# The beginning of mixer 1 in a two-layer hybrid backbone: the context's norm at other points, rotary sums in PSUM, eight scalings left out, one query copy moved

## The chip, the core and the metric

The kernel runs on one core of one Trainium2 chip. The core has a matrix engine (PE), a vector engine (DVE), a scalar engine (ACT), a general engine (POOL) and a sync engine (SP) that here issues the transfers from HBM. Each engine runs its own instructions in order and waits on semaphores for the others. SBUF holds the operands; PE writes into eight PSUM banks, which DVE and ACT read. The metric is the device time of one execution in microseconds, taken as the median of several runs; lower is better.

## The reference, cut to what matters

512 latent tokens and 256 context tokens of width 1024 pass two layers; each layer is half a SwiGLU, a token mixer and half a SwiGLU again, every one of them modulated and closed by a layer norm. Mixer 1 is windowed attention with 16 query heads, 4 key heads and rotary positions. Its context tokens give keys and values only: behind this mixer nothing reads them.

```python
def window_gqa(u_lat, u_ctx, w_qkv, w_o, sinks, with_ctx_out):
    qkv = u_lat @ w_qkv
    q = axial_rope(qkv[..., :dq].reshape(B, S, N_HEADS, HEAD_DIM)) * scale
    k = axial_rope(qkv[..., dq:dq + dkv].reshape(B, S, WA_KV_HEADS, HEAD_DIM))
    v = qkv[..., dq + dkv:].reshape(B, S, WA_KV_HEADS, HEAD_DIM)
    kvc = u_ctx @ w_qkv[:, dq:]
...
    # per block of 128 queries: softmax over a window of 384 keys, all 256 context keys and a sink
...
# in reference(), for layer i = 1 (ctx_needed is False):
        h_lat = ffn_sublayer(h_lat, m_lat[0], m_lat[1], m_lat[2], ffn_w_in[i, 0], ffn_w_out[i, 0], ln_g[i, 0], ln_b[i, 0])
        h_ctx = ffn_sublayer(h_ctx, m_ctx[0], m_ctx[1], m_ctx[2], ffn_w_in[i, 0], ffn_w_out[i, 0], ln_g[i, 0], ln_b[i, 0])
        u_lat = modulate(h_lat, m_lat[3], m_lat[4])
        u_ctx = modulate(h_ctx, m_ctx[3], m_ctx[4])
        y_lat, y_ctx = window_gqa(u_lat, u_ctx, wa_w_qkv[j], wa_w_o[j], wa_sinks[j], ctx_needed)
        h_lat = layer_norm(ALPHA * h_lat + m_lat[5] * y_lat, ln_g[i, 1], ln_b[i, 1])
        h_lat = ffn_sublayer(h_lat, m_lat[6], m_lat[7], m_lat[8], ffn_w_in[i, 1], ffn_w_out[i, 1], ln_g[i, 2], ln_b[i, 2])
```

## The kernel before

Activations lie transposed: `z[d]` holds 128 of the 1024 channels for all 768 tokens, latent columns 0 to 511, context columns 512 to 767. What a product reads is split in two parts, a high one (`uh`, `wh`) and the rest (`ul`, `wl`); a product of exact numbers is three PE products of such parts (`mm3`, L163, L165, L166). Weights come as quarters of 128x512: SP loads one into `wr` (five buffers), ACT casts it into `wh` (L102), POOL subtracts into `wl` (L104).

The functions that the change touches are in `wa_mixer` and before it. The value and key products of the latent tokens (`vw`, `wk`) run over the eight channel tiles, and the name `wa_0` to `wa_7` marks the end of each. Then `query` makes two products of the first unit (`wq0_0`, `wq0_1`); `scaled` copies a bank into SBUF on ACT (`qe`). `turned` does the rotation: PE multiplies `qe` with a permutation (`pr`, L1129), DVE multiplies that with the sines (`sn`, L1131), POOL multiplies `qe` with the cosines (L1132), DVE adds (L1133). `stack_k` and `stack_q` copy the result on ACT and make the remainder on DVE: for the keys L868, L869, L870, L871, for the queries L861, L862. Then come the context's keys (`wkc`) and values (`vw` with `wh_0b` and so on), and the first query product of the next unit (named `early` in the code, `wq_0` in the profile again). `attn` makes the scores (`sw` and `sc`, L875 and L876), their minimum on DVE (L1217, L1220) and the exponential on ACT (L1232).

The norm that feeds this mixer is `l3`: `l3[0]` for the latent tokens, `l3[1]` for the context. It has seven parts: sums, mean, centers, variance (`pvl`, L475), spreading (`prl`, L403), out (the scaled tokens: `ufl` L318, `uh` L320, L322 or L324, `ul` L325) and kept (POOL scales `z` for the residual, L339). `plan` hangs parts on named points, and `at` runs them when the program gets there. With `firm`, the first product issued behind a variance or a spreading is held behind it on PE.

A scheduler that lays out its own timeline sets the order of each engine's instructions from this program, the dependencies, the buffers and PSUM banks that come free, and orders that `behind` fixes by hand. The banks are named by tags: two each of `mm`, `s` and `c`, one each of `t` and `o`. So an instruction can move though its line was not touched.

Of the kernel before, what the change touches and what calls it, by code (L numbers as in the profile page):

```python
# [37 lines left out]
def hybrid_kernel(ctx: ExitStack, tc: tile.TileContext, h0, cc, crow, wmod, wmodt, bmod, lnp, wst,  # L38
# [129 lines left out]
    def mmk(ps, w, m0, c0, c1, k0=0):  # L168

        for k in range(DT):  # L170
            kk = (k + k0) % DT
            mm3(ps, kw(w, kk, m0, m0 + P), [t[kk][:, c0:c1] for t in (uh, ul)], k == 0, k == DT - 1)

# [691 lines left out]
    def stack_k(k0, k1, kl0, kl1, c0, c1, src):  # L865

        for k, kl, own, other in ((k0, kl0, LOW, HIGH), (k1, kl1, HIGH, LOW)):
            nc.scalar.copy(k[own, c0:c1], src[own, :])  # L868
            nc.scalar.copy(k[other, c0:c1], src[own, :])  # L869
            nc.vector.tensor_tensor(out=kl[own, c0:c1], in0=src[own, :], in1=k[own, c0:c1].bitcast(F32), op=ALU.subtract)  # L870
            nc.scalar.copy(kl[other, c0:c1], kl[own, c0:c1].bitcast(F32))  # L871
# [232 lines left out]
    def wa_mixer(gt):  # L1104
# [15 lines left out]
        def scaled(nm, ps, scale, tag="t2"):  # L1120

            qe = t2(f"qe{nm}", tag)
            nc.scalar.activation(qe[:], ps[:], AF.Copy, scale=scale)
            return qe

        def turned(nm, qe):

            pr = bank("mm", f"pr{nm}")
            nc.tensor.matmul(pr[:], rm_sb[:], qe[:], start=True, stop=True)  # L1129
            sn = t2(f"sn{nm}")  # L1130
            nc.vector.tensor_tensor(out=sn[:], in0=pr[:], in1=rc[1][:], op=ALU.mult)  # L1131
            nc.gpsimd.tensor_tensor(out=qe[:], in0=qe[:], in1=rc[0][:], op=ALU.mult)  # L1132
            nc.vector.tensor_tensor(out=sn[:], in0=qe[:], in1=sn[:], op=ALU.add)  # L1133
            return sn

        def stacked_q(nm, qe):
            sl = [ph["S"].tile([P, NL], F32R, tag="wq", name=f"w{nm}_{x}", bufs=6) for x in range(2)]
            stack_q(*sl, 0, NL, turned(nm, qe), 1.0)
# [19 lines left out]
        def query(u, wq, i, tag="t2"):  # L1158
            ps = bank("mm", f"wq{u}_{i}")
            mmk(ps[:], wq, i * P, 0, NL)  # L1160
# [16 lines left out]
        for i in range(2):  # L1177
            stack_k(*ks[i], 0, NL, turned(f"k{i}", kes[i]))
        qes.append(query(0, wq, 1))
        qs = [stacked_q("q0_0", qes[0])]  # L1180
        for i in range(2):
            ps = bank("s", f"wkc{i}")
            mmk(ps[:, :NC], w, i * P, NL, NT)
            if i == 0:
                qs.append(stacked_q("q0_1", qes[1]))
            stack_k(*ks[i], NL, NT, ps[:, :NC])
# [214 lines left out]
    l3 = [ln("l3", i, g, 1, 0, 1, 3, "o", firm=i == 0, alone=i == 1) for i, g in enumerate(g2)]  # L1401
# [15 lines left out]
    plan(wa_4=l3[1][1:3], wa_7=l3[1][3:4], wq0_0=l3[1][4:6], wq0_1=l3[0][6:] + l3[1][6:])  # L1417
# [131 lines left out]
```

## Time and profile before

| | us |
|---|---|
| median of 3 runs | 2731.77 |
| the runs | 2731.77, 2726.20, 2731.79 |
| the profiled execution, its own time | 2735.21 |
| its span in the trace | 2733.4 |
| mean granted PE clock | 0.988 |

The page's first part gives the busy time of each engine; its second part cuts the span into 40 slices of 68 us and gives the busy share in tenths. Mixer 1 begins at about 2042 us, where the latent tokens' norm is done, and its first exponential starts at 2112.97 us. In these 71 us the views by order of time show each instruction with its start, its length, its tiles, and in brackets how long its engine had been idle before it and which instruction ended that.

### The profile page before, as it was taken

The numbers are of one execution on the slowest core, as the hardware profiler recorded it, in microseconds if no ns is written. First come the engines' busy times: TensorE is split into PE (matmuls) and PEld (weight loads), VectorE is DVE, ScalarE is ACT, GpSimd is POOL, SyncE is SP. The second block draws the span as 40 slices with busy tenths as digits, with TensorE's granted clock in tenths as the row PEclk, the third lists the DMA queues.
The fourth block names the chain that finished last, engine by engine and source line by source line (L and its number), as shares of the span: only waits on it lengthen the run. The fifth ranks groups of instructions, "written<-read, shape, count | busy, mean of one in ns | idle before, by whom it ended". The sixth has DMA issues, their size and how long they took to land.

```text
span 2733.4 us, 47740 instructions
## 1 busy us (share of the span) xinstructions
PE 2635.5 (96%) x16858; PEld 2406.7 (88%) x16858; DVE 1834.8 (67%) x4268; ACT 1206.9 (44%) x2505; POOL 1667.7 (61%) x1523
## 2 busy tenths in 40 slices
PE   7999999999999899999999999999998999899997
PEld 5799999888888889999998899999987777899997
DVE  4877777775555687556556676666577767687765
ACT  5244343266446353443433534343336655454542
POOL 4786767464444567867664577767645545577762
PEclk9999999999999999999999999999999999999998
DMA  9367565422222222454543226456632111245551
GB/s 332 94 176 197 140 164 166 145 78 67 59 59 63 59 61 83 132 130 121 128 130 101 69 82 160 125 150 173 200 115 62 32 32 43 66 105 128 135 143 59
DMA packets 295759, 311.90 MB, mean 114 GB/s; under 512 B 27873, under 2 KB 194017, under 8 KB 294497
## 3 DMA queue, kind: packets, MB, share of 16 engines
q1 hardware_dynamic: 279104, 279.36, 34.3%
q0 software_dynamic: 16128, 29.37, 6.4%
q8 instruction: 133, 2.18, 0.3%
q14 instruction: 106, 0.86, 0.1%
q10 hardware_dynamic: 288, 0.14, 0.0%
HBM read 300.92 MB, written 12.25 MB: 115 GB/s over the span
## 4 chain that ended last, share of the span: by engine, by line
PE 56%; DVE 6%; ACT 2%; issue 1%; DMA 1%; POOL 0%; DVEq 0%; SPq 0%; ACTq 0%; POOLq 0%
PE pd0b L165 2%; PE pd0b L163 2%; PE pd0b L166 2%; PE pd1a L163 2%; PE pd1a L165 2%; PE pd1a L166 2%; PE pd1b L163 1%; PE wo L909 1%; PE pd1b L165 1%; PE pd1b L166 1%; DVE z L503 1%; PE tpw L899 1%; PE sw L875 0%; PE wq L163 0%; PE wq L166 0%
## 5 line engine op out<-in xcount | busy, mean ns | idle before, releaser
L104 POOL TENSOR_TENSOR wl<-wr,wh 128x512 fp32r<-128x512 f32 x200 | 261.5, 1323 | 161.3 <-ACT wh L102 88.9
L104 POOL TENSOR_TENSOR wl_s<-S,wh_s 128x512 fp32r<-128x512 f32 x240 | 316.6, 1354 | 48.9 <-ACT wh_s L102 48.5
L102 ACT CAST wh_s<-S 128x512 fp32r<-128x512 f32 x256 | 155.2, 620 | 424.3 <-POOL S L644 140.9
L644 POOL TENSOR_TENSOR S<-wr,wr 128x512 f32<-128x512 f32 x128 | 173.9, 1359 | 187.3 <-DMA wr<-in_wst_dram 170.9
L211 DVE CUSTOM_DVE_ANT_0 jk<-wt,cb 128x512 f32<-128x512 f32 x360 | 244.6, 679 | 22.5 <-DMA wt<-in_wmodt_dram 18.2
L104 POOL TENSOR_TENSOR wl_a<-wr,wh_a 128x512 fp32r<-128x512 f32 x144 | 189.0, 1359 | 18.9 <-ACT wh_a L102 16.7
L102 ACT CAST wh_a<-wr 128x512 fp32r<-128x512 f32 x192 | 119.2, 622 | 155.3 <-PE pd1b L165 20.8
L102 ACT CAST wh<-wr 128x512 fp32r<-128x512 f32 x200 | 121.1, 617 | 108.0 <-DMA wr<-in_wst_dram 17.2
L503 DVE SCALAR_TENSOR_TENSOR z<-pd0b,gt,z 128x256 f32<-128x256 f32 (+1 forms) x168 | 96.7, 594 | 38.2 <-PE pd0b L166 37.9
L503 DVE SCALAR_TENSOR_TENSOR z<-pd1a,gt,z 128x512 f32<-128x512 f32 (+1 forms) x150 | 88.6, 605 | 37.4 <-PE pd1a L166 36.6
L918 POOL TENSOR_SCALAR p<-p,l 128x512 f32<-128x512 f32 x64 | 44.3, 694 | 102.3 <-DVE l L1025 95.3
L503 DVE SCALAR_TENSOR_TENSOR z<-pd0a,gt,z 128x512 f32<-128x512 f32 (+1 forms) x160 | 93.6, 611 | 15.7 <-PE pd0a L166 15.4
L644 POOL TENSOR_TENSOR S<-wr,S 128x512 f32<-128x512 f32 x64 | 90.3, 1411 | 3.4
L644 POOL TENSOR_TENSOR S<-S,wr 128x512 f32<-128x512 f32 x64 | 90.1, 1407 | 2.9
L339 POOL TENSOR_SCALAR z<-z,ag_None,ab_None 128x256 f32<-128x256 f32 (+1 forms) x77 | 59.2, 772 | 51.6 <-DVE uh L324 32.8
L918 POOL TENSOR_SCALAR pw<-pw,l 128x512 f32<-128x512 f32 (+1 forms) x64 | 42.6, 666 | 71.4 <-DVE l L1246 41.7
L1024 ACT ACTIVATE p<-s,m 128x512 f32<-128x512 f32 x64 | 44.0, 688 | 77.8 <-DVE m L1021 70.7
L325 DVE TENSOR_TENSOR ul<-ufl,uh 128x256 fp32r<-128x256 f32 (+1 forms) x88 | 61.7, 708 | 6.0 <-ACT uh L320 3.5
L503 DVE SCALAR_TENSOR_TENSOR z<-pd1b,gt,z 128x512 f32<-128x512 f32 (+1 forms) x91 | 53.2, 618 | 9.7 <-PE pd1b L166 8.2
L318 ACT ACTIVATE ufl<-z,bi_None,sc_None 128x256 f32<-128x256 f32 (+1 forms) x77 | 48.1, 637 | 25.2 <-DVE z L488 24.9
L104 DVE TENSOR_TENSOR wl_a<-wr,wh_a 128x512 fp32r<-128x512 f32 x48 | 51.6, 1086 | 6.3 <-ACT wh_a L102 6.3
L163 PE MATMUL vn<-wh,uh 128*128 128x256 f32 x192 | 54.7, 285 | 1.1 <-DVE nq L862 0.6
(1479 smaller groups left out, 10579.1 us busy)
## 6 DMA issues: line engine op xcount, KB each, us to landing
wr<-in_wst_dram SPq DMA_DIRECT2D x456, 256.0 KB
wt<-in_wmodt_dram SPq DMA_DIRECT2D x206, 256.0 KB
wr_0b<-in_wst_dram SPq DMA_DIRECT2D x47, 256.0 KB
wr_1b<-in_wst_dram SPq DMA_DIRECT2D x47, 256.0 KB
wr_2b<-in_wst_dram SPq DMA_DIRECT2D x47, 256.0 KB
wr_3b<-in_wst_dram SPq DMA_DIRECT2D x47, 256.0 KB
wm<-in_wmod_dram SPq DMA_DIRECT2D x8, 1024.0 KB
zspare<-in_wmodt_dram SPq DMA_DIRECT2D x30, 256.0 KB
```

The source lines that it names most:

```text
L102: nc.scalar.copy(hi[:], src[:])
L104: x = eng.tensor_tensor(out=lo[:], in0=src[:], in1=hi[:].bitcast(F32), op=ALU.subtract)
L163: behind(nc.tensor.matmul(ps, a[0], b[0], start=first, stop=False), in_front[0])
L165: nc.tensor.matmul(ps, a[0], b[1], start=False, stop=False)
L166: last_pe[0] = nc.tensor.matmul(ps, a[1], b[0], start=False, stop=last)
L211: x = nc.vector.tensor_tensor_reduce(out=junk[:], in0=w[:], in1=cb[st], scale=1.0, scalar=0.0, op0=ALU.mult, op1=ALU.add, accum_out=out[st])
L318: nc.scalar.activation(uv, zs, AF.Identity, scale=s1, bias=s2)
L325: return hi, nc.vector.tensor_tensor(out=lo, in0=uv, in1=uo.bitcast(F32), op=ALU.subtract)
L339: nc.gpsimd.tensor_scalar(out=zs, in0=zs, scalar1=prm[2][:, d:d + 1], scalar2=prm[3][:, d:d + 1], op0=ALU.mult, op1=ALU.add)
L503: last[0] = nc.vector.scalar_tensor_tensor(out=zt(d, c0, c1), in0=pd, scalar=gt[:, d, st:st + 1], in1=zt(d, c0, c1), op0=ALU.mult, op1=ALU ...
L644: nc.gpsimd.tensor_tensor(out=t[:], in0=a[:], in1=b[:], op=o)
L918: nc.gpsimd.tensor_scalar(out=p, in0=p, scalar1=r, scalar2=0.0, op0=ALU.mult, op1=ALU.add)
```

## The change

In four places the program is changed. `mmk` marks a point behind each of the eight channel tiles of a product, so that a plan can name them. The context's norm `l3[1]` is issued at `wa_3` (mean, centers), `wa_6` (variance) and `wq0_0_4` (spreading, out) in place of `wa_4`, `wa_7` and `wq0_0`, and it is `firm` now; its last part, the eight scalings of the context's `z`, is left out, as nothing reads them. `turned` may be given a bank: then the permuted tile is taken in that bank and DVE leaves the product and the sum there. The two keys use `t` and `c`, the first unit's two queries `mm`. And the copy in `scaled` is held on ACT behind the last copy of `stack_k`, when there is one, which concerns the next unit's query.

```diff
@@ -165,11 +165,12 @@
         nc.tensor.matmul(ps, a[0], b[1], start=False, stop=False)
         last_pe[0] = nc.tensor.matmul(ps, a[1], b[0], start=False, stop=last)
 
-    def mmk(ps, w, m0, c0, c1, k0=0):
+    def mmk(ps, w, m0, c0, c1, k0=0, nm=None):
 
         for k in range(DT):
             kk = (k + k0) % DT
             mm3(ps, kw(w, kk, m0, m0 + P), [t[kk][:, c0:c1] for t in (uh, ul)], k == 0, k == DT - 1)
+            at(f"{nm}_{k}")
 
 
     def gemv(layer, ch, pieces, tag):
@@ -868,7 +869,8 @@
             nc.scalar.copy(k[own, c0:c1], src[own, :])
             nc.scalar.copy(k[other, c0:c1], src[own, :])
             nc.vector.tensor_tensor(out=kl[own, c0:c1], in0=src[own, :], in1=k[own, c0:c1].bitcast(F32), op=ALU.subtract)
-            nc.scalar.copy(kl[other, c0:c1], kl[own, c0:c1].bitcast(F32))
+            x = nc.scalar.copy(kl[other, c0:c1], kl[own, c0:c1].bitcast(F32))
+        return x
 
     def scores(ps, q, k, kl, qc, kc):
 
@@ -1120,22 +1122,24 @@
         def scaled(nm, ps, scale, tag="t2"):
 
             qe = t2(f"qe{nm}", tag)
-            nc.scalar.activation(qe[:], ps[:], AF.Copy, scale=scale)
+            behind(nc.scalar.activation(qe[:], ps[:], AF.Copy, scale=scale), last_k[0])
             return qe
 
-        def turned(nm, qe):
-
-            pr = bank("mm", f"pr{nm}")
+        def turned(nm, qe, room=None):
+
+            pr = bank(room or "mm", f"pr{nm}")
             nc.tensor.matmul(pr[:], rm_sb[:], qe[:], start=True, stop=True)
-            sn = t2(f"sn{nm}")
+            sn = pr if room else t2(f"sn{nm}")
             nc.vector.tensor_tensor(out=sn[:], in0=pr[:], in1=rc[1][:], op=ALU.mult)
             nc.gpsimd.tensor_tensor(out=qe[:], in0=qe[:], in1=rc[0][:], op=ALU.mult)
             nc.vector.tensor_tensor(out=sn[:], in0=qe[:], in1=sn[:], op=ALU.add)
             return sn
 
-        def stacked_q(nm, qe):
+        last_k = [None]
+
+        def stacked_q(nm, qe, room=None):
             sl = [ph["S"].tile([P, NL], F32R, tag="wq", name=f"w{nm}_{x}", bufs=6) for x in range(2)]
-            stack_q(*sl, 0, NL, turned(nm, qe), 1.0)
+            stack_q(*sl, 0, NL, turned(nm, qe, room), 1.0)
             return sl
 
         iv = wpos[0]
@@ -1157,7 +1161,7 @@
 
         def query(u, wq, i, tag="t2"):
             ps = bank("mm", f"wq{u}_{i}")
-            mmk(ps[:], wq, i * P, 0, NL)
+            mmk(ps[:], wq, i * P, 0, NL, nm=f"wq{u}_{i}")
             at(f"wq{u}_{i}")
             return scaled(f"q{u}_{i}", ps, -0.125, tag)
 
@@ -1175,15 +1179,15 @@
         wq = wunit()
         qes = [query(0, wq, 0)]
         for i in range(2):
-            stack_k(*ks[i], 0, NL, turned(f"k{i}", kes[i]))
+            stack_k(*ks[i], 0, NL, turned(f"k{i}", kes[i], "tc"[i]))
         qes.append(query(0, wq, 1))
-        qs = [stacked_q("q0_0", qes[0])]
+        qs = [stacked_q("q0_0", qes[0], "mm")]
         for i in range(2):
             ps = bank("s", f"wkc{i}")
             mmk(ps[:, :NC], w, i * P, NL, NT)
             if i == 0:
-                qs.append(stacked_q("q0_1", qes[1]))
-            stack_k(*ks[i], NL, NT, ps[:, :NC])
+                qs.append(stacked_q("q0_1", qes[1], "mm"))
+            last_k[0] = stack_k(*ks[i], NL, NT, ps[:, :NC])
         wv = wunit(again=iv)
         for j in (4, 5):
             context_v(j)
@@ -1398,7 +1402,7 @@
     l0 = [ln("l0", i, g, 0, 0, 0, 3, "o", firm=i == 0, alone=i == 1) for i, g in enumerate(g2)]
     l1 = [ln("l1", i, g, 0, 1, 0, 6, ("mm", "t", "o")[i], held=False, pool=i == 0) for i, g in enumerate(g3)]
     l2 = [ln("l2", i, g, 0, 2, 1, 0, "o", True, firm=i == 0) for i, g in enumerate(g2)]
-    l3 = [ln("l3", i, g, 1, 0, 1, 3, "o", firm=i == 0, alone=i == 1) for i, g in enumerate(g2)]
+    l3 = [ln("l3", i, g, 1, 0, 1, 3, "o", firm=True, alone=i == 1) for i, g in enumerate(g2)]
     l4 = [ln("l4", i, g, 1, 1, 1, 6, ("mm", "o")[i]) for i, g in enumerate(g1)]
 
     ffn("0a", g2, lambda: gate(0, 2, 0.5), late_gate, whole(l0[0], l0[1][:1]), first,
@@ -1414,7 +1418,7 @@
     gemv_dve(1, (24, 40, (0, 1)), (40, 72, (0,)))
     plan(pa1a_0_0_0=l2[0][6:], pa1a_0_1_0=l2[1][1:3], pd1a_0_0_1=l2[1][3:4], pd1a_0_0_4=l2[1][4:])
     ffn("1a", g2, lambda: gate(1, 2, 0.5), None, whole(l3[0], l3[1][:1]), apart=True)
-    plan(wa_4=l3[1][1:3], wa_7=l3[1][3:4], wq0_0=l3[1][4:6], wq0_1=l3[0][6:] + l3[1][6:])
+    plan(wa_3=l3[1][1:3], wa_6=l3[1][3:4], wq0_0_4=l3[1][4:6], wq0_1=l3[0][6:])
     plan(wo6_2=l4[0][:1], wo6_3=l4[0][1:2], wm7_3=l4[0][2:3], wo7_3=l4[0][3:4] + [lambda: back(last_rstd[0])],
          pow3_1_256_2=[lambda: back(None)] + l4[0][4:6], pow3_1_256_7=l4[1][:1])
     wa_mixer(gate(1, 5, 1.0))
```

The diff shifts the line numbers: a line of the program before is one to four higher in the changed one (L1129 is L1131 there, L861 is L862, L475 is L476). What the change makes of the order, on two engines. On PE at the first key's rotation, before: `wq_0` is the first query's product, `prk` the two keys' rotations.

```order
L166 MATMUL wq_0_23085<-uh_106,wl_2_23076 128x512
L475 MATMUL pvl_1_23025<-onesd,aql_1_1_22948 128x1 x2
L163 MATMUL wq_0_23085<-uh_107,wh_3_23081 128x512
L165 MATMUL wq_0_23085<-ul_115,wh_3_23081 128x512
L166 MATMUL wq_0_23085<-uh_107,wl_3_23082 128x512
L163 MATMUL wq_0_23085<-uh_108,wh_3_23081 128x512
L165 MATMUL wq_0_23085<-ul_116,wh_3_23081 128x512
L166 MATMUL wq_0_23085<-uh_108,wl_3_23082 128x512
L1129 MATMUL prk_23155<-qek_23049,rm_sb 128x512
L1129 MATMUL prk_23169<-qek_23051,rm_sb 128x512
L163 MATMUL wq_1_23183<-uh_101,wh_0_23063 128x512
```

And after, at the first key's rotation, which now stands ahead of the first query's products:

```order
L166 MATMUL wk_22847<-uh_108,wl_3_22839 128x512
L476 MATMUL pvl_1_23007<-onesd,aql_1_1_22930 128x1 x2
L163 MATMUL vw_22842<-wh_3_22814,uh_108 128x256
L165 MATMUL vw_22842<-wl_3_22815,uh_108 128x256
L166 MATMUL vw_22842<-wh_3_22814,ul_116 128x256
L1131 MATMUL prk_23155<-qek_23049,rm_sb 128x512
L163 MATMUL wq_0_23085<-uh_101,wh_0_23063 128x512
L165 MATMUL wq_0_23085<-ul_109,wh_0_23063 128x512
```

The first rotation stands ahead of all 24 products of the first query in place of behind them; the variance `pvl` stands ahead of the last three value products. The second key's rotation follows 15 query products later, and the spread (`prl`) 15 after that.

On ACT behind the last context token (`uh_108`), up to the copies of the context's keys (`wk` and `wkl` out of `wkc`), before; `wq` out of `snq` are query copies, `qeq` is the next unit's query.

```order
L102 CAST wh_3_23414<-wr_3_23412 128x512
L318 ACTIVATE ufl_1_7_23149<-z_99,bi_0_1_3_None,sc_0_1_3_None 128x256
L322 ACTIVATE uh_108<-z_99,bi_0_1_3_None,sc_0_1_3_None 128x256
L102 CAST wh_0_23964<-wr_0_23962 128x512
L102 CAST wh_1_23970<-wr_1_23968 128x512
L1123 ACTIVATE qeq_0_23443<-wq_0_23418 128x512
L868 CAST wk_0_23041<-wkc_23238 64x256
L869 CAST wk_0_23041<-wkc_23238 64x256
L102 CAST wh_2_23976<-wr_2_23974 128x512
L868 CAST wk_1_23045<-wkc_23283 64x256
L869 CAST wk_1_23045<-wkc_23283 64x256
```

And after, at the same place:

```order
L323 ACTIVATE uh_108<-z_99,bi_0_1_3_None,sc_0_1_3_None 128x256
L102 CAST wh_2_23396<-wr_2_23394 128x512
L102 CAST wh_3_23402<-wr_3_23400 128x512
L862 ACTIVATE wq_0_0_23216<-prq_0_23218 64x512
L102 CAST wh_0_23952<-wr_0_23950 128x512
L102 CAST wh_1_23958<-wr_1_23956 128x512
L862 ACTIVATE wq_0_1_23217<-prq_0_23218 64x512
L869 CAST wk_0_23041<-wkc_23227 64x256
L862 ACTIVATE wq_1_0_23252<-prq_1_23254 64x512
L870 CAST wk_0_23041<-wkc_23227 64x256
L102 CAST wh_2_23964<-wr_2_23962 128x512
L869 CAST wk_1_23045<-wkc_23271 64x256
```

The next unit's query (`qeq`) no longer stands ahead of the context's keys, and the first unit's query copies, which stood ahead of the last context tokens, stand among the weight casts behind them.

On PE at the end of the context's products, before: `wkc` and `vw` are the context's keys and values, `wq_0` is the next unit's first query.

```order
L165 MATMUL vw_23367<-wl_3b,uh_108 128x256
L166 MATMUL wq_0_23418<-uh_107,wl_3_23415 128x512
L163 MATMUL wq_0_23418<-uh_108,wh_3_23414 128x512
L165 MATMUL wq_0_23418<-ul_116,wh_3_23414 128x512
L166 MATMUL wq_0_23418<-uh_108,wl_3_23415 128x512
L165 MATMUL wkc_23238<-ul_116,wh_3_22838 128x256
L166 MATMUL wkc_23238<-uh_108,wl_3_22839 128x256
L165 MATMUL wkc_23283<-ul_116,wh_3_22838 128x256
L166 MATMUL wkc_23283<-uh_108,wl_3_22839 128x256
L166 MATMUL vw_23340<-wh_3b,ul_116 128x256
L166 MATMUL vw_23367<-wh_3b,ul_116 128x256
L875 MATMUL sc_1_0_23508<-wk_0_23041,wq_0_0_23226 128x256
```

And after:

```order
L165 MATMUL vw_23328<-wl_3b,uh_108 128x256
L166 MATMUL vw_23328<-wh_3b,ul_116 128x256
L166 MATMUL vw_23355<-wh_3b,ul_115 128x256
L163 MATMUL vw_23355<-wh_3b,uh_108 128x256
L165 MATMUL vw_23355<-wl_3b,uh_108 128x256
L166 MATMUL vw_23355<-wh_3b,ul_116 128x256
L163 MATMUL wq_0_23406<-uh_101,wh_0_23384 128x512
L165 MATMUL wq_0_23406<-ul_109,wh_0_23384 128x512
L166 MATMUL wq_0_23406<-uh_101,wl_0_23385 128x512
```

The 24 products of that query stood among the context's products and now stand behind all of them. In the last FFN, where the same norm helper serves the latent tokens, the scheduler has moved one spread (`prl`) ahead of 12 products; no line of it was changed.

## The prediction, made before the changed kernel was run

> **What bounds the kernel now.** I read the totals by engine first, then the busy time in stretches of 10 us over the beginning of mixer 1, then the order of time of PE, ACT, DVE and POOL there.
>
> ```profile
> PE 2635.5 (96%) x16858; PEld 2406.7 (88%) x16858; DVE 1834.8 (67%) x4268; ACT 1206.9 (44%) x2505; POOL 1667.7 (61%) x1523
> ...
> 2080.00:2090.00 10.00, 7.02 (x32) 5.16 (x31) 9.07 (x15) 9.77 (x18) 7.08 (x7) 0.83 0.30 78
> ...
> 2100.00:2110.00 10.00, 6.59 (x37) 5.27 (x36) 5.44 (x8) 6.04 (x16) 7.44 (x6) 1.00 0.45 132
> 2110.00:2120.00 10.00, 7.47 (x27) 6.01 (x26) 7.41 (x30) 6.83 (x20) 2.42 (x4) 0.50 0.07 26
> ```
>
> A stretch's row gives busy us of PE, weight loads, DVE, ACT and POOL, then the granted clock. PE is busy 96% of the span, so only places where it waits can be won, and these three stretches are such a place: PE 7.02, 6.59 and 7.47 of 10, ACT at 9.77 in the first, and the clock down to 0.83 and 0.50. The waits themselves (start, us, idle before and releaser in brackets):
>
> ```profile
> 2072.44 1.98 PE L1129 MATMUL prk<-qek,rm_sb 128*128 128x512 f32 x4
> ...
> 2078.49 0.60 PE L403 MATMUL prl<-idn,yl 128*128 128x128 f32 x4
> ...
> 2085.31 0.38 PE L165 MATMUL wkc<-ul,wh 128*128 128x256 f32 x1 [2.92 <-DVE ul L325]
> ...
> 2086.56 0.41 PE L163 MATMUL vw<-wh_0b,uh 128*128 128x256 f32 x1
> 2086.77 0.41 PE L165 MATMUL vw<-wl_0b,uh 128*128 128x256 f32 x1
> ...
> 2090.31 0.28 PE L165 MATMUL vw<-wl_1b,uh 128*128 128x256 f32 x1
> 2090.43 0.28 PE L163 MATMUL vw<-wh_1b,uh 128*128 128x256 f32 x1
> ...
> 2104.49 0.40 PE L166 MATMUL vw<-wh_3b,ul 128*128 128x256 f32 x2
> 2105.50 0.38 PE L875 MATMUL sc<-wk,wq 128*128 128x256 f32 x1 [0.61 <-ACT wk L869]
> 2108.12 0.38 PE L876 MATMUL sc<-wkl,wq 128*128 128x256 f32 x1 [2.24 <-ACT wkl L871]
> ...
> 2113.80 0.69 PE L875 MATMUL sw<-wk,wq 128*128 128x384 f32 x1 [1.97 <-ACT pw L1232]
> ```
>
> Two waits matter. At 2085.31 the context's products stop 2.92 us for the context's normed tokens; afterwards equal products start 0.21 us apart instead of 0.12, the halved clock. From 2104.9 the first scores wait, step after step, for ACT's copies of the context's keys. ACT's rows say why those are late:
>
> ```profile
> 2076.67 0.62 ACT L868 CAST wk<-snk 64x512 fp32r<-64x512 f32 x1 [0.29 <-DVE snk L1133]
> 2077.32 0.62 ACT L869 CAST wk<-snk 64x512 fp32r<-64x512 f32 x1
> ...
> 2099.07 1.39 ACT L102 CAST wh<-wr 128x512 fp32r<-128x512 f32 x2 [0.81 <-PE wkc L165]
> 2104.22 0.60 ACT L1123 ACTIVATE qeq<-wq 128x512 f32<-128x512 f32 x1 [3.77 <-PE wq L166]
> ...
> 2109.94 0.87 ACT L871 CAST wkl<-wkl 64x256 fp32r<-64x256 f32 x2
> 2111.67 1.28 ACT L1232 ACT_TABLE_LOAD   x1 [0.86 <-DVE m L1220]
> 2112.97 0.69 ACT L1232 ACTIVATE pw<-sw,m 128x512 f32<-128x512 f32 x1
> ```
>
> From the first key cast (2076.67) to the last (2110.8) ACT waits only twice, 0.81 and 3.77 us. ACT is the bound of this stage; the 3.77 us are the query copy that stood ahead of the key copies while its products were not done. I take the exponential at 2112.97 as the stage's end.
>
> **The change, step by step.** All times on the clock of before.
>
> *Rotated keys.* They now start as soon as their product is there:
>
> ```profile
> 2066.01 1.29 ACT L1123 ACTIVATE qek<-wk 128x512 f32<-128x512 f32 x2
> ...
> 2066.28 0.39 PE L166 MATMUL wk<-uh,wl 128*128 128x512 f32 x1
> 2066.51 0.39 PE L163 MATMUL wq<-uh,wh 128*128 128x512 f32 x1
> ...
> 2073.54 2.55 POOL L1132 TENSOR_TENSOR qek<-qek,rc 128x512 f32<-128x512 f32 x2 [6.16 <-PE prk L1129]
> ...
> 2073.50 0.69 DVE L1131 TENSOR_TENSOR snk<-prk,rc 128x512 f32<-128x512 f32 x1 [0.41 <-PE prk L1129]
> ...
> 2075.06 3.28 DVE L1133 TENSOR_TENSOR snk<-qek,snk 128x512 f32<-128x512 f32 x2
> ```
>
> PE spends 0.23 us on a product of 512 columns (2066.28 to 2066.51), 0.12 on one of 256. Three value products move behind the keys, so the first key's last product starts at 2066.28 - 0.36 - 0.69 = 2065.2 and ends at 2065.6; ACT's copy (1.29/2) ends at 2066.3; PE meanwhile does the second key (0.69), the variance (0.3) and three value products (0.36) and comes to the rotation at 2066.8, unhindered. Rotation 1.0, POOL's product 1.28, DVE's sum and three handovers of 0.1 follow. The sum took 1.64 us (3.28/2) with both operands in SBUF; the row at 2073.50, with one operand in PSUM and POOL busy beside it, took 0.69. With the sum left in PSUM I take 0.69, and 1.64 as the other end. ACT's first key cast: 2070.2 instead of 2076.67, **6.5 us earlier** (5.5 by the other end).
>
> *ACT's chain.* It lasted 2110.8 - 2076.7 = 34.1 us. Out go both waits (4.6) and the query copy (0.5); in come a weight cast that stood ahead (0.65, a cast's pitch from 2076.67 to 2077.32) and one wait for DVE's residual, as the first key's low copy now stands directly behind its casts:
>
> ```profile
> 2078.26 1.40 DVE L870 TENSOR_TENSOR wkl<-snk,wk 64x512 fp32r<-64x512 f32 x2
> ```
>
> That is 1.40/2 + 0.05 = 0.75. So 30.4 us, and its end at 2100.6, 10.2 earlier. Reading PSUM rather than SBUF could change its 12 rotated casts and copies by 0.05 us each either way: 0 taken, +-0.6 as bounds.
>
> *The context's norm.* Its variance comes at about 2066.2 on PE, and its reciprocal root, which ended at 2074.3 (first row below), some 4 us earlier. PE goes: first rotation done 2067.8, 30 query products (6.9), second rotation (1.0), so the spread at 2075.7 instead of 2078.49, not waiting; 18 more query products (4.1) and the spread (0.4): context at 2080.2, its first low half needed six products later, at 2080.9.
>
> ```profile
> 2074.11 0.15 DVE L367 SCALAR_TENSOR_TENSOR yl<-pvl,yl 128x2 f32<-128x2 f32 x1
> ...
> 2083.71 1.54 DVE L325 TENSOR_TENSOR ul<-ufl,uh 128x256 fp32r<-128x256 f32 x1 [0.83 <-ACT ufl L318]
> ...
> L339 POOL TENSOR_SCALAR z<-z,ag_None,ab_None x8: 659/874/1240, 2085.0 to 2100.8; 128x256 f32<-128x256 f32 x8
> ```
>
> Ahead of the context's first scaling ACT has 13 casts (13 x 0.64) and the 0.75: 2079.3, scaled 2079.8; DVE's last key residual and the low half (0.7 + 0.4, or 1.54 as in its row) end at 2080.6 to 2081.7. PE waits 0 to 0.8 us here instead of 2.92; I take 0, as POOL has no work then. The 96 products (11.5) and two rotations (1.9) run at full clock to 2093.6. POOL's eight unread scalings (8 x 0.87 = 7.0 us) go; nothing waited for them, so 0, at best what they held up on DVE.
>
> *The new wait.* The first query's sum now stays in the bank that the next query's 24 products need; they wait for DVE's second residual of it. ACT ends the last context token at 2090.2 by its chain, then come two weight casts, a query copy, two weight casts, a query copy: 6 x 0.64, 2094.1; DVE 0.7: 2094.8. **PE waits 1.2 us**; queued behind are those 24 products (5.5), ending at 2100.3, then the scores (12 x 0.12 and a drain): 2102.
>
> *The first exponential.* DVE's new order puts both heads' masks ahead of both minima:
>
> ```profile
> 2111.87 0.49 DVE L1217 CUSTOM_DVE_ANT_0 sw<-sw,mk,nsink 128x256 f32<-128x256 f32 x1 [0.28 <-PE sw L876]
> ```
>
> So one mask, one minimum (0.5 each) and reads (0.3) behind the scores, 2103.3; table load 1.28: 2104.6 against 2112.97. **-8.4 us.** Behind it the order is the old one, and PE at 96% with weights fetched on request carries the shift to the end.
>
> *A second place.* In the last FFN the same norm helper's spread moves ahead of 12 products (1.4 us):
>
> ```profile
> 2362.17 0.60 PE L403 MATMUL prl<-idn,yl 128*128 128x128 f32 x4
> ...
> 2364.71 0.39 PE L163 MATMUL pa1b<-uh,wh 128*128 128x256 f32 x1 [1.22 <-ACT uh L320]
> ```
>
> The 1.22 us wait that follows should mostly go: -1.0, between -1.2 and +0.3 (if the root isn't ready).
>
> Sum -9.4 us. Of the profiled execution's 2735.21 (span 2733.4 and 1.8 around it) that leaves 2725.8. That execution lies 3.4 us above the median 2731.77; on the median **2722.4**. What a measurement of this kernel can tell from no change is about 0.2%, 5.5 us.
>
> **Rivals.**
>
> *Carried only in part.* For: ACT has no slack between 2070 and 2100, so whatever it waits for adds in full. Weight quarters are asked for when POOL is done with the fifth one before, and took 3.2 us:
>
> ```profile
> 2067.41 0.33 SPq L94 DMA_DIRECT2D wr<-in_wst_dram  x1
> ...
> 2067.40:2070.60 3.20, 3.20 (x16) 2.64 (x15) 0.00 (x0) 0.00 (x0) 0.00 (x0) 1.00 0.34 90
> ```
>
> The quarter cast at 2092.8 is asked for at 2089.4 by my walk and there at 2092.6: margin 0.2. With ACT 4 to 7 us behind, -2.5 to -5.4. Against: the old chain had no wait for a DMA.
>
> *It doesn't do what it says*, or attention gives it back to a wait that no order shows: 0 to -2.5, 2729 to 2732. Against: the stage behind keeps its order.
>
> *Slower: the clock at the new bank wait.* After 2.92 us of idle PE ran 4 us at half clock (0.21 for 0.12), a loss near 2 us. My wait is 1.2. If the second residual comes after 2096.5, the wait reaches 2.9 and the 24 products run slow: every us of ACT's lateness counts, and 2 more on top. It ends slower than before once ACT is 7.4 us late: with a quarter 15 us late, the price is 15 + 2 - 9.4, about +8, 2739. Nothing in the profile shows a quarter so late.
> The Trainium skill ("TensorE: Matmul & The Clock Gate", Part 1) says that the clock halves after an idle window of about 3.4 us and returns after as long a busy one. By that rule a wait of 1.2 would cost no clock, as here taken; this trace had it after 2.92.
>
> *The other way*: the half-clock stretch from 2110 to 2120 (0.50) may go with the waits ahead of it: up to half of PE's 7.47 busy us, -3.7. The new order still leaves PE idle from 2102 to 2105.2, so I take 0.
>
> **How the numbers follow.** The forecast, -6 to -13: 0.62. In part: 0.16, a quarter of it over 5.5. Not carried: 0.15. Slower: 0.07. Faster by over 0.2%: 0.62 + 0.04 = 0.66; within: 0.27; slower: 0.07. The low end is -9.4 - 3.7 and 3 for the spread of the runs shown (2726.2 to 2731.79): 2716; the high end takes in the partial cases to -1: 2731.
>
> **What would show it.** Right: the first rotation 5 us ahead of the second, no wait over 1 us at the context's first low halves, a clock near 1.0 from 2080 to 2090, a wait of about 1 us at the second unit's first query product, and the first exponential near 2104.6. Wrong: the context's low halves again waiting for ACT's scalings, ACT waiting for a quarter's DMA, or the exponential no earlier than 2109.

## The result, and the profile after

The changed kernel took 2717.27 us, the median of 6 runs (2714.30 to 2723.84), against 2729.56 for the kernel before beside it (6 runs, 2722.59 to 2731.79). The ratio is 0.9952, 95% interval 0.9934 to 0.9971: between 8 and 18 us faster. The forecast was 9.4 us off the median of 2731.77, to 2722.4; the two medians here lie 12.3 apart. The profiled execution has a span of 2722.1 us (time 2723.84), mean clock 0.991.

Busy time by stretches of 10 us, columns as in the prediction. Everything lies 1.9 us later than before by then, since the stage's first value product starts at 2045.41 and not at 2043.47.

```profile
2080.00:2090.00 10.00, 10.00 (x67) 8.69 (x66) 7.72 (x16) 9.91 (x21) 4.77 (x4) 1.00 0.31 83
2090.00:2100.00 10.00, 9.74 (x63) 8.70 (x63) 8.19 (x13) 9.03 (x21) 10.00 (x9) 1.00 0.51 141
2100.00:2110.00 10.00, 5.98 (x31) 4.59 (x30) 5.87 (x24) 7.76 (x21) 2.46 (x3) 0.91 0.28 72
2110.00:2120.00 10.00, 10.00 (x82) 8.95 (x81) 6.65 (x29) 6.68 (x24) 4.87 (x9) 0.75 0.01 2
```

PE, at 7.02 of 10 us and clock 0.83 in the first stretch before, is busy all through it at full clock. PE in order of time:

```profile
2045.41 0.39 PE L163 MATMUL vw<-wh,uh 128*128 128x256 f32 x1 [1.25 <-ACT uh L321]
...
2068.90 1.02 PE L1131 MATMUL prk<-qek,rm_sb 128*128 128x512 f32 x2
...
2073.19 1.02 PE L1131 MATMUL prk<-qek,rm_sb 128*128 128x512 f32 x2
...
2082.73 0.28 PE L165 MATMUL wkc<-ul,wh 128*128 128x256 f32 x1
...
2095.79 0.50 PE L163 MATMUL wq<-uh,wh 128*128 128x512 f32 x1 [0.26 <-DVE wq L863]
...
2102.68 0.28 PE L878 MATMUL sw<-wkl,wq 128*128 128x256 f32 x1
```

The rotations stand 4.3 us apart, the context's first low half (2082.73) is not waited for, and the new wait at the bank is 0.26 us. ACT:

```profile
2072.06 0.58 ACT L869 CAST wk<-prk 64x512 fp32r<-64x512 f32 x1 [1.79 <-DVE prk L1135]
...
2073.98 0.62 ACT L872 CAST wkl<-wkl 64x512 fp32r<-64x512 f32 x1 [0.75 <-DVE wkl L871]
...
2093.54 0.62 ACT L102 CAST wh<-wr 128x512 fp32r<-128x512 f32 x1 [0.51 <-DMA wr<-in_wst_dram]
2094.42 0.59 ACT L862 ACTIVATE wq<-prq 64x512 fp32r<-64x512 f32 x1 [0.26 <-DVE wq L863]
...
2101.43 0.88 ACT L872 CAST wkl<-wkl 64x256 fp32r<-64x256 f32 x2
2102.33 0.60 ACT L1125 ACTIVATE qeq<-wq 128x512 f32<-128x512 f32 x1
2104.03 1.28 ACT L1236 ACT_TABLE_LOAD   x1 [1.10 <-DVE m L1224]
2105.32 0.69 ACT L1236 ACTIVATE pw<-sw,m 128x512 f32<-128x512 f32 x1
```

From its first value product to the first exponential the stage now lasts 2105.32 - 2045.41 = 59.9 us; before it was 2112.97 - 2043.47 = 69.5. **The stage is 9.6 us shorter.** The span is 11.3 us shorter: +1.9 ahead of the stage (the same program without the hold, below, begins it at 2040.8), -9.6 in it, +1.4 to the last score, -5.7 from there to mixer 1's last output product (`pow`), +0.7 behind that. The -5.7 looks like a second gain. These are that piece's stretches, of before, then of the changed kernel:

```profile
2314.70:2339.20 24.50, 20.93 (x130) 17.90 (x129) 14.95 (x52) 10.89 (x27) 11.70 (x14) 0.65 0.17 44
```

```profile
2308.50:2327.30 18.80, 14.85 (x130) 11.91 (x129) 14.59 (x51) 10.36 (x27) 11.17 (x14) 1.00 0.17 45
```

The same 130 products, DVE, ACT and POOL alike, but PE at a clock of 0.65 before and 1.00 after. Whether the change brought that or the moment of the run is the first thing the experiments had to tell.

### The profile page after: what moved, and what is told of

It reads as the page before. It is cut to its first block, busy times and chain, and to the rows that moved or that the text cites. A ratio compares the mean times of both kernels' runs of the same rounds, so it can differ in the third digit from the quotient of the medians.

```text
span 2722.1 us, 47725 instructions
## 1 busy us (share of the span) xinstructions
PE 2632.6 (97%) x16858; PEld 2406.2 (88%) x16858; DVE 1835.4 (67%) x4268; ACT 1206.5 (44%) x2505; POOL 1666.3 (61%) x1515
## 4 chain that ended last, share of the span: by engine, by line
PE 55%; DVE 6%; ACT 1%; DMA 1%; issue 1%; POOL 0%; SPq 0%; DVEq 0%; ACTq 0%; POOLq 0%
PE pd0b L163 2%; PE pd0b L165 2%; PE pd0b L166 2%; PE pd1a L163 2%; PE pd1a L165 2%; PE pd1a L166 2%; PE wo L911 1%; DMA wr<-in_wst_dram 1%; PE pd1b L163 1%; PE pd1b L165 1%; PE pd1b L166 1%; DVE z L504 1%; PE tpw L901 1%; DVE sw L1221 1%; PE wq L163 0%
## 5 line engine op out<-in xcount | busy, mean ns | idle before, releaser
L102 ACT CAST wh<-wr 128x512 fp32r<-128x512 f32 x200 | 120.8, 617 | 98.6 <-DMA wr<-in_wst_dram 18.9
L340 POOL TENSOR_SCALAR z<-z,ag_None,ab_None 128x256 f32<-128x256 f32 (+1 forms) x69 | 52.3, 762 | 51.7 <-DVE uh L325 32.6
```

The source lines that it names most:

```text
L102: nc.scalar.copy(hi[:], src[:])
L340: nc.gpsimd.tensor_scalar(out=zs, in0=zs, scalar1=prm[2][:, d:d + 1], scalar2=prm[3][:, d:d + 1], op0=ALU.mult, op1=ALU.add)
```

## The experiments

One timing here has an interval of +-0.14 to 0.23%, 4 to 6.3 us, so single parts are read in the trace: stage, as above, and the start of ACT's first key copy behind the stage's start. The stage starts with mixer 1's first value product, which is one of the latent tokens; the expectations below call it the context's.

| kernel | first key copy, us | stage, us | ratio to before, interval |
|---|---|---|---|
| before | 33.2 | 69.5 | |
| changed | 26.7 | 59.9 | 0.9952 (0.9934 to 0.9971) |
| changed, no hold | 26.7 | 60.0 | 0.9966 (0.9950 to 0.9982) |
| changed, scalings kept | 26.7 | 60.9 | 0.9957 (0.9941 to 0.9974) |
| changed, all sums in SBUF | 34.6 | 63.8 | 0.9988 (0.9967 to 1.0009) |
| changed, norm late | 32.6 | 63.4 | 0.9986 (0.9969 to 1.0003) |
| before, hold alone | 33.2 | 70.5 | 1.0025 (1.0008 to 1.0042) |
| before, scalings left out alone | 33.2 | 71.2 | 1.0008 (0.9990 to 1.0026) |
| before, sums in PSUM alone | 32.6 | 63.4 | 0.9992 (0.9975 to 1.0009) |
| before, norm alone | 34.5 | 64.3 | 1.0001 (0.9978 to 1.0024) |
| changed, query sums in SBUF | 26.6 | 63.1 | 0.9961 (0.9946 to 0.9975) |
| changed, table loaded early | 26.7 | 59.0 | 0.9956 (0.9941 to 0.9970) |
| changed, three copies on POOL | 26.6 | 59.1 | 0.9959 (0.9942 to 0.9975) |
| changed, both of these | 26.7 | 57.9 | 0.9951 (0.9933 to 0.9970) |

### One part taken out of the change

**No hold**, the query's copy not fixed behind the key copies:

```diff
-            behind(nc.scalar.activation(qe[:], ps[:], AF.Copy, scale=scale), last_k[0])
+            nc.scalar.activation(qe[:], ps[:], AF.Copy, scale=scale)
```

> The changed kernel without the condition that holds the query's scaled copy behind the last key copy. Measured in the trace: the stage, from the start of the context's first value product to the start of mixer 1's first exponential (69.5 us before, 59.9 changed), and the rest, from there to the end of the span (620.4 before, 616.8 changed). Mine: the other parts put the copy at that place already, PE and ACT have the same instructions in the same order, so the stage is 59.9 within 0.5 and the ratio of times is 0.995 as with the change. Rival A, the hold itself saves a copy's time ahead of the keys (0.6 to 1.3 us on ACT): stage 60.5 to 61.2. Rival B, of the 3.6 us that the rest is shorter a part is only where the half-clock windows fall from run to run: then the rest differs here from 616.8 by 2 us or more although the program is the same.

Stage 60.0, so with the other parts the hold does nothing. The program is the changed one, instruction for instruction on PE, ACT, DVE and POOL. The rest, from the exponential to the end, is 614.0 us here and 616.8 in the changed kernel: one and the same program differs by 2.8 us there, as rival B has it.

**Scalings kept**, so that the unread products are made again:

```diff
-    plan(wa_3=l3[1][1:3], wa_6=l3[1][3:4], wq0_0_4=l3[1][4:6], wq0_1=l3[0][6:])
+    plan(wa_3=l3[1][1:3], wa_6=l3[1][3:4], wq0_0_4=l3[1][4:6], wq0_1=l3[0][6:] + l3[1][6:])
```

> The changed kernel with POOL's eight scalings of z put back (8 x 0.88 = 7.0 us, four of them ahead of the query's first multiplication). Mine: POOL waits 4.8 us for ACT there and hides them; stage 59.9 within 1, ratio 0.995. Rival: with POOL busy all the time from 2084 to 2101 the last of the four and the four behind them delay the query's rotations and the low halves of the next unit's weights, so the next unit's products and the scores come 2 to 4 us later: stage 62 to 64, ratio 0.996 to 0.997; the removed work would then be a real part of the gain.

60.9, at the edge of my band: the scalings are worth 0.9 us of stage, not nothing. ACT's wait for a weight quarter, 0.51 in the changed kernel, is 1.73 here, and PE waits 1.40 at the bank for 0.26:

```profile
2092.43 0.62 ACT L102 CAST wh<-wr 128x512 fp32r<-128x512 f32 x1 [1.73 <-DMA wr<-in_wst_dram]
```

```profile
2094.44 0.50 PE L163 MATMUL wq<-uh,wh 128*128 128x512 f32 x1 [1.40 <-DVE wq L863]
```

This kernel and the kernel before with the scalings left out settle the 5.7 us. The piece from the last score to the last `pow`, of the one and of the other:

```profile
2305.20:2329.50 24.30, 20.82 (x129) 17.77 (x128) 14.90 (x52) 10.74 (x27) 11.29 (x14) 0.66 0.17 45
```

```profile
2322.90:2341.60 18.70, 14.75 (x130) 11.85 (x129) 14.48 (x51) 10.31 (x27) 10.99 (x14) 1.00 0.16 44
```

With nearly the whole change the piece is slow, with the old order on PE it is quick. Nor do the scalings decide it: with them made, it takes 18.7 in the kernel before with sums in PSUM alone, and with them left out 24.3 in the changed kernel with three copies on POOL. In all 14 profiles the length goes with how long the trace's clock record shows half speed there. From start to start (the rows above have rounded ends) it is 18.7 without any, 18.9 with 3.4 us of it, 20.5 with 6.8, 22.8 and 23.0 with 10.2 and 13.7, 24.3 to 24.5 with 17.1 (all stretches that reach into the piece added up, also where some of one lies outside). **So the -5.7 in the two profiles is no effect of the change**; of their 11.3 us, the stage's 9.6 are, and a wait that is gone in the last FFN, of which below.

**All sums in SBUF:**

```diff
-            stack_k(*ks[i], 0, NL, turned(f"k{i}", kes[i], "tc"[i]))
+            stack_k(*ks[i], 0, NL, turned(f"k{i}", kes[i]))
-        qs = [stacked_q("q0_0", qes[0], "mm")]
+        qs = [stacked_q("q0_0", qes[0])]
-                qs.append(stacked_q("q0_1", qes[1], "mm"))
+                qs.append(stacked_q("q0_1", qes[1]))
```

> The changed kernel with all four first rotary sums written to SBUF again. Mine: the key sums beside POOL's work go from 0.7 back to about 1.6 us, each of two 0.9 later on the chain that feeds ACT's key copies, and the copies from SBUF 0.62 for 0.58; the key rotations also are issued 15 to 18 PE products later, behind the norm's spread: the first key copy 2 to 4 us later, stage 62 to 64, ratio 0.996 to 0.997; the wait for the bank ahead of the next unit's query product goes (0.3). Rival: ACT's chain is set by the norm, not by the key sums: stage 59.9 to 60.5.

63.8, within my band, but the first key copy comes 7.9 us later and the stage loses only 3.9. My reason, the key chain that feeds ACT, is not borne out by that. The edit also changes the order on PE, the key rotations standing behind the norm's spread again, so the 3.9 us are order and price of the sums together.

**Norm late:**

```diff
-    l3 = [ln("l3", i, g, 1, 0, 1, 3, "o", firm=True, alone=i == 1) for i, g in enumerate(g2)]
+    l3 = [ln("l3", i, g, 1, 0, 1, 3, "o", firm=i == 0, alone=i == 1) for i, g in enumerate(g2)]
-    plan(wa_3=l3[1][1:3], wa_6=l3[1][3:4], wq0_0_4=l3[1][4:6], wq0_1=l3[0][6:])
+    plan(wa_4=l3[1][1:3], wa_7=l3[1][3:4], wq0_0=l3[1][4:6], wq0_1=l3[0][6:])
```

> The changed kernel with the context's norm issued at the old, coarser points. Mine: the first key rotation goes back behind all query products and the norm's spread 12 products back, so the first key copy and the norm's scalings on ACT come 3 to 5 us later: stage 63 to 65, ratio 0.996 to 0.9975, and PE waits again 1 to 3 us at the context's first low halves. Rival: the norm's place does not count once the sums stay in PSUM: stage 59.9 to 61, ratio 0.995.

63.4, as expected; but PE waits only 0.43 us at the context's first low half, not 1 to 3. This kernel and the kernel before with the sums in PSUM alone, below, differ in the scalings and the hold only; key copy and stage are the same in both, so with the norm late neither of these counts.

### One part alone, on the kernel before

The edits are the change's own for each part, the other parts left as before.

> The kernel before with only the query's copy held behind the key copies. Stage (first value product of the context to mixer 1's first exponential) before 69.5 us, changed 59.9. Mine: ACT takes its 25 or so copies in another order, the first key copies come one copy (1.3 us at most) earlier and the query's rotation some 8 us later, whose room is until the scores: stage 68.5 to 69.5, ratio 0.9995 to 1. Rival: the query's late copy delays the scores: stage 70 to 72, ratio 1.0005 to 1.001.

70.5, which is the rival's number, but not for its reason. ACT waits 4.00 us for the key product itself, so the copy that had stood ahead of it cost nothing:

```profile
2099.44 0.37 ACT L869 CAST wk<-wkc 64x256 fp32r<-64x256 f32 x1 [4.00 <-PE wkc L166]
```

The 1.0 us more come from the clock. Up to the end of PE's wait of 2.92 us the two kernels run alike, 41.8 us behind the stage's start; but then this one is at half clock until 2084.86, and the same products on PE come 0.96 later:

```profile
2079.34 0.58 PE L165 MATMUL wkc<-ul,wh 128*128 128x256 f32 x1 [2.92 <-DVE ul L326]
```

```profile
2078.00:2084.90 6.90, 5.56 (x21) 4.68 (x21) 6.05 (x9) 6.75 (x14) 4.44 (x5) 0.51 0.27 76
```

The half clock lasts 6.8 us here, from within the wait on. In the kernel before it lasted 3.4, from 2086.09, which is 0.8 behind the end of the wait. The hold by itself does nothing that the trace shows.

> The kernel before with only POOL's eight scalings left out (the same order on the other engines). Mine: nothing on the chain; stage 69.5 within 1, ratio 1.000. Rival: POOL shares something with VectorE, and 7.0 us less of POOL's work make VectorE's operations beside it shorter (1.64 to about 0.7 for a sum): stage 66 to 68, ratio 0.998 to 0.9995.

71.2, above both bands. PE waits 2.93 us at the context's low halves as before, then 0.80 and 0.73 at two later ones, where it had waited 0 and 0.26. The order on PE, ACT and DVE is that of before. The trace shows what less of POOL's work did: without the scalings POOL gets to the remainders of the next weights (`wl`) some 2 us earlier, and there they fall beside DVE's sum of the second query and the low half for which PE waits. Here, POOL and DVE:

```profile
2097.40 3.17 POOL L104 TENSOR_TENSOR wl<-wr,wh 128x512 fp32r<-128x512 f32 x2
...
2097.98 1.45 DVE L1135 TENSOR_TENSOR snq<-qeq,snq 128x512 f32<-128x512 f32 x1
2099.35 1.50 DVE L326 TENSOR_TENSOR ul<-ufl,uh 128x256 fp32r<-128x256 f32 x1
...
2100.91 0.38 PE L165 MATMUL wkc<-ul,wh 128*128 128x256 f32 x1 [0.80 <-DVE ul L326]
```

The same two DVE operations in the kernel before, beside two of the scalings:

```profile
2091.50 1.95 POOL L339 TENSOR_SCALAR z<-z,ag_None,ab_None 128x256 f32<-128x256 f32 x2
...
2092.05 0.72 DVE L1133 TENSOR_TENSOR snq<-qeq,snq 128x512 f32<-128x512 f32 x1
2092.69 0.41 DVE L325 TENSOR_TENSOR ul<-ufl,uh 128x256 fp32r<-128x256 f32 x1
```

They take 2.95 us for 1.13. Of these 1.8 us, 1.3 come out as PE's waits (0.80, and 0.73 for 0.26), and the masks add 0.3: most of the 1.7. So the rival's view, that DVE's time hangs on what POOL does beside it, is right, and its sign wrong: what counts is which operations meet.

> The kernel before with only the four first rotary sums left in PSUM (the key rotations take banks of other groups than the query's products). Mine: each key sum 0.7 for 1.6 us, the key copies 0.9 to 2 us earlier: stage 66 to 68.5, ratio 0.9985 to 0.9995. Rival: most of the gain lies in this part alone, since the rotations no longer share a ring of banks: stage 60 to 63, ratio 0.9955 to 0.997.

63.4, outside both bands, but close to the rival's 60 to 63 and far from mine, with the first key copy only 0.6 us earlier. The old wait of 2.92 us is almost gone, although the norm is issued late:

```profile
2088.81 0.39 PE L165 MATMUL wkc<-ul,wh 128*128 128x256 f32 x1 [0.43 <-DVE ul L326]
```

At a later low half PE waits 0.64. With the rotations in other banks PE's order changes, too: the next unit's 24 query products stand behind all of the context's products now, as in the changed kernel. So it isn't shown how much of the 6.1 us is the price of the sums and how much the order.

> The kernel before with only the norm issued at the finer points. Mine: the spread 28 products earlier, the first key rotation 9 earlier, the low halves of the context's norm ready before PE needs them (PE's wait of 2.92 us goes): stage 63 to 66, ratio 0.9965 to 0.998. Rival: without the sums in PSUM the norm's scalings stand ahead of the key copies on ACT and only change places with them: stage 68 to 69.5, ratio 0.9993 to 1. The four single parts add up to the change's 9.6 us of stage if they are independent; if the parts need one another, the sum of the singles is well under it.

64.3, as expected; the wait there is 1.16. The singles add up to -6.1 - 5.2 + 1.0 + 1.7 = -8.6 against -9.6, but that sum is no test, since the 1.0 is the clock's. The two large parts bring 6.1 and 5.2 alone, each over half, and 8.6 together, which is "scalings kept" (the hold does nothing there): they overlap by 2.7. Leaving out the scalings is worth 0.9 beside both, nothing beside the sums in PSUM without the finer norm, and costs 1.7 alone.

The times hold more than the stage. In the last FFN the scheduler puts the spread (`prl`) at one of several places though no edit touches it, and the wait behind it is 1.22 us before, with the scalings left out alone, with three copies on POOL and with both versions; 1.93 with all sums in SBUF, with the norm late, and with hold, sums or norm alone; and gone in the others. With stage and this wait added, every interval fits but that of the hold alone: 2 to 11 us slower, of which 1.0 is the stage's clock and 0.7 this wait. The rest stays open.

### Which sums count

Query sums in SBUF again, key sums in PSUM (the last two edits of "all sums in SBUF"):

> The changed kernel with the two query sums written to SBUF again and the two key sums still in PSUM; the order on the engines stays that of the change. Stage (first value product of the context to mixer 1's first exponential): 59.9 us changed, 63.8 with all four sums in SBUF. Mine: the key sums are worth most of the 3.9, since they feed ACT's first key copies; the query's operations in SBUF beside POOL's work cost 0.6 to 0.9 more each, four of them in the stretch 2086 to 2096 where VectorE is busy nearly all the time, less the bank wait of 0.3 that goes: stage 60.5 to 62. Rival: the query sums are the part that counts, since the scores come last: stage 62.5 to 64. Other rival: the bank wait of the changed kernel eats what the query sums bring: stage 59.5 to 60.2.

63.1: the rival's. The first key copy is as early as in the changed kernel, and yet 3.2 of the 3.9 us are lost. PE and POOL have the changed kernel's order; on ACT and DVE some of the query's copies and residuals stand elsewhere. By its time this kernel can't be told from the changed one, so the reading rests on the stage alone. DVE's groups in the stage, here:

```profile
L863 DVE SCALAR_TENSOR_TENSOR wq<-snq,wq 64x512 fp32r<-64x512 f32 x4 | 5.4, 1346 | 0.1
L1135 DVE TENSOR_TENSOR snq<-qeq,snq 128x512 f32<-128x512 f32 x2 | 3.5, 1727 | 0.0
```

and in the changed kernel:

```profile
L863 DVE SCALAR_TENSOR_TENSOR wq<-prq,wq 64x512 fp32r<-64x512 f32 x4 | 2.8, 689 | 0.9 <-ACT wq L862 0.8
L1135 DVE TENSOR_TENSOR prq<-qeq,prq 128x512 f32<-128x512 f32 x2 | 1.4, 680 | 0.0
```

Behind the line comes busy time and the mean of one in ns. The four residuals of the queries take 1.35 us each out of SBUF and 0.69 out of PSUM, the two sums 1.73 and 0.68: 4.7 us of DVE's work, and ACT then waits for DVE:

```profile
2102.62 1.29 ACT L862 ACTIVATE wq<-snq 64x512 fp32r<-64x512 f32 x2 [2.09 <-DVE snq L1135]
```

POOL was busy 9.55 and DVE 9.93 of the 10 us ahead of that wait:

```profile
2090.00:2100.00 10.00, 8.77 (x63) 7.64 (x62) 9.93 (x11) 8.59 (x17) 9.55 (x7) 1.00 0.38 107
```

The Trainium skill ("SBUF — State Buffer", section "SBUF: two separate sides") says that a VectorE operation with two SBUF inputs and a GpSimd operation that reads SBUF hold a shared port exclusively, and the later one is blocked. The doubled means agree with that, and so does their going once one operand is in PSUM.

### Two versions beyond the change

**Table loaded early.** A one-column exponential that nothing reads, behind the last key copy:

```diff
         early = query(1, wq, 0, "ln")
+        wt = small("le", "lewarm")
+        behind(nc.scalar.activation(wt[:, 0:1], nsink[:, 0:1], AF.Exp, scale=1.0), last_k[0])
```

> The changed kernel with an exponential of one column, whose result is not read, on ACT behind the last key copy, so that ACT loads the table of the exponential (1.28 us) while it would wait 1.1 us for the first minimum. Mine: ACT's last key copy ends at 2102.3 on the changed kernel's clock, load, small exponential (about 0.25) and the query's copy (0.6) end at 2104.45; the first exponential starts there and not at 2105.3: stage 59.0 to 59.2, 0.7 to 0.9 less; ratio 0.995 or 0.0003 under that of the change, below what the times can tell. Rival: another function between the two needs the old table, which is loaded once more (a fifth and sixth load in the trace's list): stage 60 to 62.

59.0, as expected (the unrounded gain is 0.96), and there is still one table load for the stage.

**Three copies on POOL:**

```diff
-    def stack_k(k0, k1, kl0, kl1, c0, c1, src):
+    def stack_k(k0, k1, kl0, kl1, c0, c1, src, pool=()):
...
-            x = nc.scalar.copy(kl[other, c0:c1], kl[own, c0:c1].bitcast(F32))
+            put = nc.gpsimd.tensor_copy if own in pool else nc.scalar.copy
+            x = put(kl[other, c0:c1], kl[own, c0:c1].bitcast(F32))
...
-            stack_k(*ks[i], 0, NL, turned(f"k{i}", kes[i], "tc"[i]))
+            stack_k(*ks[i], 0, NL, turned(f"k{i}", kes[i], "tc"[i]), (LOW, HIGH)[1 - i:])
```

> The changed kernel with three of the four copies of the local keys' low halves to the other half of the partitions (ACT, 0.62 each, the three behind 2078) made by POOL. Mine: ACT's chain sets the stage, POOL has 4.8 us of waiting for ACT ahead of the third low half of the values' weights, and three copies of 0.6 to 1.3 fit in it: ACT's last key copy 1.9 us earlier, stage 58.0, between 57.4 and 59. Rival: POOL, busy without a gap from 2084 to 2101 in the changed kernel, sets the stage as much as ACT; the copies delay the low halves of the weights and ACT's 1.9 us turn into waits: stage 59.9 to 62.

59.1, just outside my band: of 1.9 us taken from ACT, 0.8 come out. ACT now waits 1.07 us for a query's sum, where it had not waited:

```profile
2084.95 0.59 ACT L862 ACTIVATE wq<-prq 64x512 fp32r<-64x512 f32 x1 [1.07 <-DVE prq L1136]
...
2096.34 1.28 ACT L1237 ACT_TABLE_LOAD   x1 [1.45 <-DVE m L1225]
```

In the changed kernel, in the last 9.8 us ahead of PE's wait at the bank, PE, DVE, ACT and POOL are each busy for 9.0 us or more, and DVE (the third value) most:

```profile
2085.90:2095.70 9.80, 9.63 (x70) 8.45 (x68) 9.67 (x14) 9.00 (x19) 9.17 (x7) 1.00 0.40 110
```

The chain that ends last in the trace runs through ACT up to 2085.5, then through DVE, with one query copy of ACT between, to the residual that ends PE's wait, then through PE's 24 products and the scores. ACT has hardly more room: its last key copy ends about 0.1 us before a score needs it. So work taken from ACT helps only as far as DVE can follow.

**Both:**

> The changed kernel with both: the table of the exponential loaded early by an exponential of one column, and three copies of the local keys' low halves on POOL. Stage (first value product of the context to mixer 1's first exponential): 59.9 us changed, 59.0 with the early load alone, 59.1 with the three copies on POOL alone. Mine: with the copies on POOL, ACT waits 1.45 us for the first minimum and loads the table (1.28) behind it; load, small exponential (0.2) and the query's copy (0.6) need 2.1 and end about when the minimum comes, so the first exponential starts 1.2 earlier than with the copies alone: stage 57.9, the gains add. Rival: once ACT waits for VectorE, they don't add: stage 58.6 to 59.1. The ratio of times is 0.9945 to 0.996, either way not to be told from that of the change.

57.9: the gains add, 2.1 for 1.0 and 0.8; with the copies on POOL the early load is worth 1.3. Table load, small exponential and query copy run on without a wait up to the exponential:

```profile
2091.47 1.28 ACT L1198 ACT_TABLE_LOAD   x1
2092.77 0.20 ACT L1198 ACTIVATE lewarm<-nsink 128x1 f32<-128x1 f32 x1
2092.99 0.60 ACT L1126 ACTIVATE qeq<-wq 128x512 f32<-128x512 f32 x1
2093.60 0.69 ACT L1239 ACTIVATE pw<-sw,m 128x512 f32<-128x512 f32 x1
```

In the stage this version beats both kernels, by 11.6 and 2.1 us; its ratio of 0.9951 cannot be told from the change's 0.9952.

## Why the prediction was right, and where it was not

*Rotated keys.* Forecast 6.5 us earlier; counted from the stage's start 33.2 became 26.7, 6.5 earlier. The sum took 0.70 where 0.69 was taken.

*ACT's chain.* Forecast 30.4 us from the first key copy to the last, with one wait of 0.75; it is 2102.31 - 2072.06 = 30.25, and the wait 0.75. That the two agree so closely is partly luck: two waits that the walk didn't have, 0.51 and 0.26, stand against copies about 0.9 shorter in sum. The casts out of PSUM take 0.58 for 0.62, the -0.05 that stood as a bound. The walk also took a query copy (0.5) out of the chain, though two stand in it after as before. A quarter was late, for which the walk had left 0.2: it cost 0.51, the rival "in part" at a small size.

*The context's norm.* No wait where 2.92 was, as taken. But one cause that the step did not name does as much as the norm's new points: with the sums in PSUM alone the wait is 0.43 (and 0.64 at a later low half), with the norm alone 1.16.

*The scalings.* Taken at 0, "at best what they held up on DVE"; 0.9 us of the stage in the changed kernel, and 1.7 the other way when they alone go.

*The new wait.* This is the mis-sized term: 1.2 forecast, 0.26 measured. PE came to it when expected (2095.55, which is 2093.6 on the clock of before), but the residual was there 1.0 earlier, since ACT's last context token ended 1.1 earlier than the 2090.2 of my walk. The other 0.94 went through to the exponential; the 0.2 to 0.3 left of the 1.2 us by which the stage beats its forecast (9.6 for 8.4) lie at the masks and minima.

*The second place.* The wait of 1.22 us in the last FFN is gone, but the stretch from the first down product (`pd1b`) to the last `pa1b` took 47.2 before and 47.9 after: 6.8 us at half clock fell into it, here the changed kernel's row:

```profile
2342.90:2390.80 47.90, 47.39 (x367) 46.99 (x368) 33.84 (x87) 21.53 (x52) 33.95 (x35) 0.93 0.33 89
```

Without hold, the same program, at clock 1.00 throughout, it took 45.9: -1.3, beside the -1.0 taken.

```profile
2337.50:2383.40 45.90, 45.03 (x369) 44.21 (x370) 33.62 (x88) 21.40 (x52) 34.36 (x36) 1.00 0.34 92
```

*The clock.* The halved stretch at 2086 went with the wait; by the clock record it was 3.4 us long, not 4. The one behind the exponential stayed, 6.8 us for the 7.1 that lay there before, and from the exponential to the last score the changed kernel took 1.4 us longer. No gain shows there, as the 0 taken for it has it, and no loss of clock at the new bank wait.

*The number.* The medians lie 12.3 us apart for a forecast of 9.4, and the traces account for the stage's 9.6 and about 1.2 in the last FFN. That a median of 2717.27 stands 1.3 above the low end of the range, 2716, is no more than the interval of 8 to 18 us allows.

*What the forecast had right for too narrow a reason.* It let all of the stage follow from ACT's chain, and that from the keys' earlier start. With the keys as early and the query sums in SBUF, 3.2 us are lost; with the sums in PSUM and the keys 6 us later, 6.1 of 9.6 are there. The step counted the price of the keys' sums, and left out that the query sums and the residuals that read them become cheaper too. It also put the bound at ACT throughout; from 2085.9 on the chain ran through DVE, which that cheaper work relieves.

*What stays open:* how much of the stage's gain reaches the end; what else makes the hold alone slower; and what the sums in PSUM are worth in the kernel before apart from the order that comes with them. The intervals of the four kernels with all sums in SBUF, the norm late, sums alone or norm alone hold both a full carry and none. That with the query sums in SBUF lies below 1, so some of its gain is carried; those with all of the gain (0.9951 to 0.9966) fit a full carry. That the query sums count for more than the keys' is read in the stage; the times don't tell it.

## What to carry to other kernels

Where two engines are nearly full and their operations on SBUF lengthen each other, as the sums and residuals here, an operand left in PSUM can make each operation that reads it cheaper, not only the one that was looked at: count all its readers. For the same reason work taken from one of them need not be a gain; it moves what is left beside other work. In a stage where several engines are nearly full, an experiment that moves the chain's start alone tells less than one that keeps the start and changes the work. And before a difference between two profiles is put down to a change, compare the clock of the stretch in which it lies.

## What the hardware showed that was not expected

The half-clock stretches inside the program last 3.4, 6.8, 10.2 or 13.7 us in every profile (a longer one stands only at the very end), and they start and end, within a profile, on a grid of 3.413 us. The Trainium skill ("TensorE: Matmul & The Clock Gate", Part 1) describes a free-running window of 3413 ns; the record agrees. PE need not be idle for as long as that: a wait of 2.92 or 2.93 us came with 3.4 us of half clock in the kernel before and with the scalings left out alone, and with 6.8 us in the one with the hold alone, which cost 1.0 us of its stage. What half clock did to this kernel is the surprise: the same products from the last score on took 18.7 us in one profile and 24.3 in another, whatever the kernel. And a load of ACT's table, 1.28 us, can be put into a wait by an exponential of one column (0.20 us) without a second load.
